# Cosine-similarity attention on one core: another order of the instructions, another polynomial for one chunk, other places for the root steps

## The chip, the cores and the metric

The kernel runs on one core of a Trainium2 chip. The core has five engines that run their own streams of instructions in order and wait for each other through semaphores: TensorE (PE, matrix products), VectorE (DVE), ScalarE (ACT, exponentials), GpSimd (POOL) and SyncE (SP, which here issues the DMA transfers). Data come from HBM to the on-chip SBUF by DMA; PE writes its products to PSUM. The metric is the device time of one execution in microseconds (us); the lower the better.

## The reference

Q, K and V are 8 batches × 12 heads × 512 rows × 64 columns, in 32-bit floating point; tau is 0.1.

```python
Q_norm = Q / (np.linalg.norm(Q, axis=-1, keepdims=True) + 1e-10)
K_norm = K / (np.linalg.norm(K, axis=-1, keepdims=True) + 1e-10)
scores = np.einsum('bhqd,bhkd->bhqk', Q_norm, K_norm) / tau
weights = np.exp(scores - np.max(scores, axis=-1, keepdims=True))
weights = weights / (np.sum(weights, axis=-1, keepdims=True) + 1e-10)
return np.einsum('bhqk,bhkd->bhqd', weights, V).astype(np.float32)
```

As the rows are normalised, a score is at most 10, and the kernel takes the exponential without subtracting the maximum.

## The kernel before

The 96 heads are taken in 48 pairs, numbered s = 0 to 47. The first and the last pair have special code. For each pair in between the steps are these; the short names are those of the program, and the lines those of the profile.

- SP loads Q and K of the pair (LD, L315) into one of 17 buffers `qk`, and V (LV, L318) into one of 9 buffers `vf`; much later it stores the result (ST, L582) from one of 8 buffers `ob`.
- POOL squares Q and K (SQ, L341), writes V as bf16 with a column of ones beside it (VC, L553), and scales most K by their roots (SCL with w = 1, L427).
- PE adds up squares in pairs of columns (SSQ, L358), and DVE reduces them to sums per row (RED, L365 and L369).
- DVE makes the reciprocal roots by Newton's method (NEW, L394 to L403): a first value from the bits of the sum, then multiplications. These steps are made for a group of pairs at once: groups of one, then two, then four pairs. The sums x and the intermediate t lie in PSUM (`nps`), the root y in SBUF (`ys`). DVE scales Q (SCL with w = 0, L427).
- PE transposes Q and K (TR, L433), and DVE copies them to SBUF (EVA, L441, `qt`).
- PE makes the scores in four chunks c of 128 keys (SCO, L532: two matmuls, one for each head, into one of two score buffers in PSUM). ACT takes the exponential of a chunk, 128 × 1024 values (EXP, L548, `et`).
- PE multiplies the weights with V (PV, L565: for each head four pieces of four matmuls each; the column of ones gives the sum of the weights). DVE takes the reciprocal (RCP, L576) and multiplies (NRM, L578) into `ob`.

One chunk, (43,3), isn't made by ACT: DVE and POOL compute its exponential as a polynomial in six steps (Y, L488 to L490), and its pair's Q is scaled by one more step on DVE (UNIT, L418) so that the polynomial works on a suitable unit.

In the head, before the first data have come, PE runs eight dummy matmuls (L191) on the eye matrix `ident` and on a zeroed operand `warm_in`, which DVE sets to zero (L195).

No loop sets the order in which an engine takes these steps. Each step is entered once in a list, with what it needs; `ORDER` then holds for each engine a sequence of numbers of that list, and the engine runs them in this sequence. So SP also holds back whatever stands behind a transfer whose buffer is not free yet. The numbers of buffers stand in `RINGS`.

Of the kernel before, what the change touches and what calls it, by code (L numbers as in the profile page):

```python
# [108 lines left out]
def bass_cosine_similarity_attention_kernel(  # L109
# [14 lines left out]

    R_QK, R_V, R_SQ, R_QN, R_QT, R_ET, R_O, R_X = RINGS
# [13 lines left out]
    ys = [sb(f"ys{i}", [128, 64], f32) for i in range(R_X)]  # L139
    xs = {g: sb(f"xs{g}", [128, 64], f32) for g in NORM_ON_ACT}  # L140
    rk = [sb(f"rk{i}", [128, 32], f32) for i in range(R_X)]
# [3 lines left out]
    warm_in = sb("warm_in", [128, SEQ], bf16)  # L145
# [5 lines left out]
    o_ps = [nc.alloc_psum_tensor(f"ops{b}", [128, 512], f32) for b in range(2)]  # L151
    t_ps = nc.alloc_psum_tensor("tps", [128, 2, NT, 128], bf16)
    x_ps = t_ps[:, :, :, :].rearrange("p w t x -> p (w t x)").bitcast(f32)
    t_k0 = o_ps[0][:, :].bitcast(bf16)[:, 0:SEQ].rearrange("p (t x) -> p t x", t=NT)
    n_ps = nc.alloc_psum_tensor("nps", [128, R_X, 160], f32)
# [16 lines left out]

    def src(x, s):
        b, h = divmod(2 * s, NHEAD)
        return x[b, h : h + 2].rearrange("h (p t) d -> p h (t d)", t=NT)

    def key(name, s, *rest):
# [9 lines left out]
        vb[:, :, :, :, DIM : DIM + 1].rearrange("p r c h o -> p (r c h o)"), 1.0))  # L187

    def warm(e):
        for k in range(WARM):  # L190
            last = e.matmul(out=o_ps[1][:, :], lhsT=ident[:, :], rhs=warm_in[:, :], start=True, stop=True)  # L191
        return last

    P.fill = lambda e, n: e.matmul(out=o_ps[1][:, 0:n], lhsT=ident[:, :], rhs=warm_in[:, 0:n], start=True, stop=True)
    P.add("wz", "dve", "sm_dve", -100, [], lambda e: e.memset(warm_in[:, :], 0.0))  # L195
    P.add("warm", "pe", "warm", -100, ["eye", "wz"], warm)
# [5 lines left out]
    def due_red(s):  # L202
        return due_sq(s) + 2.0
# [3 lines left out]
    off_of = {s: c for s, c in OFF}  # L207
    turn_user = {}
    for (s, c), (turns, _) in OFF.items():
        for h in range(2):  # L210
            turn_user.setdefault(turns[h], []).append((s, h))
# [10 lines left out]
    for s, w in sorted(early):  # L222
        session[s, w] = (w, due_red(s), before[w])
        before[w] = [("RED", s, w)]
# [6 lines left out]
    def head0(TF):  # L231
        for h in range(2):
            at = -100 + h
            x4 = [xs[0][:, 8 * w + 4 * h : 8 * w + 4 * h + 4] for w in range(2)]
            y4 = [ys[0][:, 8 * w + 4 * h : 8 * w + 4 * h + 4] for w in range(2)]
# [7 lines left out]
            r_ps = sc_ps[:, 1, 0:4] if h == 0 else n_ps[:, 0, 128:132]  # L243
# [42 lines left out]
    def new(g):  # L286
        if g <= 0:
            return []
        return [("NEW", g, 7)] if direct_r(g) else [("NEW", g, 6), ("NEW", g, 7)]
# [7 lines left out]
    def last_direct(s):  # L297
        d = [g for g in NORM_ON_ACT if g > 0]
        return [("NEW", max(d), 7 if direct_r(max(d)) else 6)] if d and group[s] not in NORM_ON_ACT and s < 12 else []

    def pair(s):
# [6 lines left out]
        for w, x in ((0, Q), (1, K)):  # L308
            if s == 0:
# [7 lines left out]
        P.add(("LV", s), "sp", "ld", s + VLAG, [key("VC", s - R_V)],  # L317
              lambda e: e.dma_start(out=vf[iv][:, :, :], in_=src(V, s)), slot=f"v{iv}")  # L318
# [30 lines left out]
        x2 = (xs[g][:, 0 : 2 * m] if acts else n_ps[:, g % R_X, 0 : 2 * m]).rearrange("p (w x) -> p w x", w=2)  # L349
        for w in range(2):  # L350
# [16 lines left out]
            else:  # L367
# [6 lines left out]
        rq_g, rk_g = n_ps[:, g % R_X, 128 : 128 + m], xs[g][:, m : 2 * m] if acts else rk[g % R_X][:, 0:m]  # L374
        rkd = n_ps[:, g % R_X, 128 + m : 128 + 2 * m] if acts else tg[:, m : 2 * m]
        on_dve = [i for i in range(first[g], first[g] + sizes[g]) if i in K_ON_DVE]
        free = [[("SCL", i, k) for i in range(first[g - R_X], first[g - R_X] + sizes[g - R_X])] if g > R_X else []
                for k in range(2)]
        reds = [("RED", i, w) for i in range(first[g], first[g] + sizes[g]) for w in range(2)]
        if s == first[g] and g in NORM_ON_ACT:  # L380
            at = NORM_ON_ACT[g]
            P.add(("LOG", g), "act", "ln", at, reds + ["eps"],
                  lambda e: e.activation(out=ys[g % R_X][:, 0 : 2 * m], in_=xs[g][:, 0 : 2 * m], func=ACT.Ln, bias=eps[:, :]))
            direct = direct_r(g)
            P.add(("NEW", g, 7), "act", "sm_act", at + 0.01, [("LOG", g)] + ([("SCL", first[g] - 1, w) for w in range(2)] if direct and g > 1 else [("NRMS", 0, 0, 1), ("SCL", 0, 0, 1)]),
                  lambda e: e.activation(  # L386
                      out=n_ps[:, g % R_X, 128 : 128 + 2 * m] if direct else xs[g][:, m : 2 * m],
                      in_=ys[g % R_X][:, 0 : 2 * m] if direct else ys[g % R_X][:, m : 2 * m], func=ACT.Exp, scale=-0.5)).own = True
            if not direct:
                P.add(("NEW", g, 6), "act", "sm_act", at + 0.005, [("LOG", g), ("SCL", 0, 0, 1)],  # L390
                      lambda e: e.activation(
                          out=n_ps[:, g % R_X, 128 : 128 + m], in_=ys[g % R_X][:, 0:m], func=ACT.Exp, scale=-0.5)).own = True
        elif s == first[g]:
            yx = lambda e: e.tensor_tensor(out=tg, in0=xg, in1=yg, op=ALU.mult)  # L394
            yyx = lambda e: e.scalar_tensor_tensor(  # L395
                out=tg, in0=tg, scalar=-0.5, in1=yg, op0=ALU.mult, op1=ALU.mult)

            def up(dst, lo, hi):
                return lambda e: e.scalar_tensor_tensor(
                    out=dst, in0=tg[:, lo:hi], scalar=1.5, in1=yg[:, lo:hi], op0=ALU.add, op1=ALU.mult)  # L400

            steps = [
                lambda e: e.tensor_scalar(  # L403
                    out=yg.bitcast(i32), in0=xg.bitcast(i32), scalar1=-0.5, scalar2=MAGIC,
                    op0=ALU.mult, op1=ALU.add),
                yx, yyx, up(yg, 0, 2 * m), yx, yyx, up(rq_g, 0, m), up(rk_g, m, 2 * m)]
            if on_dve:
                steps.append(up(tg[:, m : 2 * m], m, 2 * m))
            for k, step in enumerate(steps):
                needs = [("NEW", g, min(k, 6) - 1 if k < 8 else 7)] if k else reds + (free[1] if K_ON_DVE else [])  # L410
                if k == 0 and g == R_X:
                    needs += [("NRMS", 0, w, h) for w in range(2) for h in range(2)]
                if 6 <= k < 8:
                    needs += free[k - 6]
                P.add(("NEW", g, k), "dve", "new", TF - 4.9 - slack(s, M_NEW) + (M_STEP * (k - 7) if s > 8 else 0.23 * k), needs, step)

        if s in off_of:
            P.add(("UNIT", s), "dve", "new", TF - 3.0, [("NEW", g, 6)], lambda e: e.tensor_scalar(  # L418
                out=rq_g[:, c8 : c8 + 8], in0=rq_g[:, c8 : c8 + 8], scalar1=UNIT * inv_tau / math.log(2.0), scalar2=1.0,
                op0=ALU.mult, op1=ALU.mult))  # L420
        for w in range(2):
# [4 lines left out]
                  [("NEW", g, (7 if direct_r(g) else 6) if acts and dve else 6 + w + (dve and w))] + ([("UNIT", s)] if s in off_of and w == 0 else []) + ([("TR", 0, w, 0), ("TR", 0, w, 1)] if s == R_QN else [key("TR", s - R_QN, w)]),  # L426
# [26 lines left out]
    def last_step(s, c):  # L453
        return {"A": 5, "B": 4, "C": 5, "P": 6}[OFF[s, c][1]]

# [9 lines left out]
    def poly(s, c, at):  # L465

        turns, form = OFF[s, c]
# [20 lines left out]
        add = lambda o, x, v: lambda e: e.tensor_scalar(out=o, in0=x, scalar1=v, scalar2=1.0, op0=ALU.add, op1=ALU.mult)  # L488
        mul = lambda o, x, y: lambda e: e.tensor_tensor(out=o, in0=x, in1=y, op=ALU.mult)
        fused = lambda o, x, v, y: lambda e: e.scalar_tensor_tensor(out=o, in0=x, scalar=v, in1=y, op0=ALU.add, op1=ALU.mult)  # L490
        steps = [("pool", "yt", mul(z, z, z)), ("pool", "ys", add(w, z, a1)), ("pool", "yt", mul(w, w, w))]
        if form == "A":
            steps += [("pool", "ys", add(w, w, a2)), ("dve", "yd", fused(e_, z, a3, w)), ("dve", "ym", mul(e_, e_, p2))]
        elif form == "B":
            steps += [("dve", "yd", fused(z, z, a3, p2)), ("dve", "yd", fused(e_, w, a2, z))]
        elif form == "C":
            steps += [("pool", "ys", add(z, z, a3)), ("pool", "yt", mul(z, z, p2)), ("dve", "yd", fused(e_, w, a2, z))]
        else:
            steps += [("pool", "ys", add(z, z, a3)), ("pool", "yt", mul(z, z, p2)), ("pool", "ys", add(w, w, a2)), ("pool", "yt", mul(e_, w, z))]
        for j, (eng, kind, step) in enumerate(steps):  # L500
# [3 lines left out]
            if j == (4 if form == "A" else last_step(s, c)):  # L504
                needs += [key("PV", s - R_ET, h, NT - 1) for h in range(2)]
            P.add(("Y", s, j), eng, kind, at + 2 + 1.9 * j, needs, step)

    def rest(s):
        iq, iv, iqt, iet, io = (s % r for r in (R_QK, R_V, R_QT, R_ET, R_O))
        T0 = START + PERIOD * s  # L510
        last_pair = s == NP - 1
        for c in range(NT):
# [3 lines left out]
            if s == 0:  # L516
                for h in range(2):
# [7 lines left out]
                              out=et[iet][:, c, h, :], in_=sc_ps[:, c, :], func=ACT.Exp, scale=xs[0][:, 8 + 4 * h + c : 9 + 4 * h + c])).own = True  # L525
# [267 lines left out]
```

## Time and profile before

| | us |
|---|---|
| three runs | 190.22, 189.85, 191.28 |
| their median | 190.22 |
| the profiled execution (its span) | 190.9 |
| busy: PE, DVE, ACT, POOL | 175.9, 170.2, 182.7, 161.8 |

The profile is of one execution. "Busy" is the time in which an engine had an instruction running. A row of a timeline gives start, duration, engine, line, operation, what it writes and reads, and how many such instructions it joins; a bracket at its end is the time in which the engine stood idle ahead of it and what ended that. A row of a table of lines gives the busy time, the mean of one in nanoseconds, and the idle time ahead. A row of a table of windows gives the busy time of each engine in that stretch, and at its end the clock that PE was granted (1.00 is full speed), the share of the DMA engines that was busy, and the bytes per second. Matmul durations overlap, so the time that PE needs for one is best read from the starts of two neighbouring rows.

### The profile page before, as it was taken

Reading aid. Unit: us, or ns where it says so; the run is one execution under the profiler, and the core shown is the slowest. Engines: PE = TensorE matmul, PEld = TensorE weight load, DVE = VectorE, ACT = ScalarE, POOL = GpSimd, SP = SyncE. Lnnn points to the kernel's source line nnn. Section 1 sums busy time; section 2 is a strip of 40 time slices with the busy share of each in tenths; the row PEclk is TensorE's granted clock in tenths of the full one; section 3 lists DMA queues with packets and bytes.
Section 4 is the critical chain, followed back from the end, with each engine's and each line's share of the span. In section 5 each row is a group of like instructions: output and inputs, shape, how many; then the busy total and the mean of one; then the engine's idle time right before and its main releaser. Section 6 shows DMA issues by size and latency. Waiting matters only on the chain.

```text
span 190.9 us, 6650 instructions
## 1 busy us (share of the span) xinstructions
PE 175.9 (92%) x2705; PEld 109.4 (57%) x2705; DVE 170.2 (89%) x552; ACT 182.7 (96%) x215; POOL 161.8 (85%) x150
## 2 busy tenths in 40 slices
PE   7699699999999999999999999999999899897973
PEld 2355266666656666666566666556656565464642
DVE  2668999999999999999997998999999999988642
ACT  5678999999999999999999999999999999999994
POOL 5397898999999999999999999999999994793000
PEclk9958999999999999999999999999999999999998
DMA  5999999997999599999979999999950414000565
GB/s 162 344 348 349 350 348 372 365 297 250 268 351 337 169 260 320 357 366 369 380 277 272 351 377 364 354 379 384 365 194 5 165 58 165 3 0 3 193 197 165
DMA packets 52446, 50.76 MB, mean 266 GB/s; under 512 B 3136, under 2 KB 52416, under 8 KB 52416
## 3 DMA queue, kind: packets, MB, share of 16 engines
q1 hardware_dynamic: 51984, 50.02, 79.7%
q8 instruction: 21, 0.34, 0.8%
q10 hardware_dynamic: 432, 0.33, 0.5%
q14 instruction: 9, 0.07, 0.1%
HBM read 37.75 MB, written 12.58 MB: 264 GB/s over the span
## 4 chain that ended last, share of the span: by engine, by line
ACT 89%; PE 4%; DMA 3%; DVE 1%; issue 0%; SPq 0%
ACT et L548 88%; DMA qk<-in_Q_dram 3%; PE ops L358 2%; PE scps L521 1%; PE tps L433 1%; DVE qn L427 1%; PE scps L532 0%; SPq L312 0%; ACT et L543 0%; ACT sq L333 0%; ACT ob L608 0%; PE tps L270 0%; DVE qn L261 0%; DVE ob L612 0%; PE ops L593 0%
## 5 line engine op out<-in xcount | busy, mean ns | idle before, releaser
L548 ACT ACTIVATE et<-scps 128x1024 bf16<-128x1024 f32 x186 | 171.3, 1113 | 0.6 <-PE scps L532 0.4
L341 POOL TENSOR_TENSOR sq<-qk 128x1024 bf16<-128x1024 f32 x44 | 83.1, 1896 | 0.1
L532 PE MATMUL scps<-qt 64*128 64x512 bf16 x374 | 73.3, 387 | 6.3 <-ACT et L548 3.3
L565 PE MATMUL ops<-vb,et 128*128 128x65 bf16 x1504 | 72.8, 195 | 1.7 <-DVE ob L578 1.0
L565 PEld LDWEIGHTS ops<-vb,et 128*128 128x128 bf16 x1504 | 55.3, 98 | 30.9 <-issue 18.3
L427 POOL TENSOR_TENSOR qn<-qk,rk 128x512 bf16<-128x512 f32 x38 | 39.5, 1045 | 5.9 <-PE scps L532 3.7
L578 DVE TENSOR_TENSOR ob<-ops,rd 128x256 f32<-128x256 f32 x94 | 38.8, 418 | 0.7
L427 DVE TENSOR_TENSOR qn<-qk,nps 128x512 bf16<-128x512 f32 x56 | 37.2, 677 | 0.7 <-ACT nps L386 0.6
L433 PE MATMUL tps<-ident,qn 128*128 128x128 bf16 x376 | 34.3, 222 | 0.9 <-POOL qn L427 0.3
L441 DVE COPY qt<-tps 128x1024 bf16<-128x1024 bf16 x47 | 32.1, 682 | 0.4 <-PE tps L433 0.4
L532 PEld LDWEIGHTS scps<-qt 64*128 64x128 bf16 x374 | 18.2, 92 | 23.5 <-ACT et L548 9.6
L369 DVE TENSOR_REDUCE nps<-sq 128x8 f32<-128x512 bf16 x46 | 30.8, 682 | 0.8 <-POOL sq L341 0.7
L553 POOL TENSOR_SCALAR vb<-vf 128x512 bf16<-128x512 f32 x48 | 29.7, 630 | 0.1
L433 PEld LDWEIGHTS tps<-ident,qn 128*128 128x128 bf16 x376 | 21.9, 99 | 12.0 <-issue 5.4
L576 DVE RECIPROCAL rd<-ops 128x4 f32<-128x4 f32 x94 | 16.1, 174 | 6.6 <-PE ops L565 5.9
L358 PE MATMUL ops<-sq,ident 128*128 128x64 bf16 x384 | 20.0, 199 | 0.1
L358 PEld LDWEIGHTS ops<-sq,ident 128*128 128x128 bf16 x384 | 15.2, 101 | 4.3 <-issue 2.5
L365 DVE TENSOR_REDUCE nps<-ops 128x8 f32<-128x64 f32 x46 | 10.0, 218 | 0.9 <-PE ops L358 0.7
L394 DVE TENSOR_TENSOR nps<-nps,ys 128x32 f32<-128x32 f32 (+2 forms) x34 | 7.0, 207 | 0.4
L395 DVE SCALAR_TENSOR_TENSOR nps<-nps,ys 128x32 f32<-128x32 f32 (+2 forms) x34 | 7.0, 206 | 0.4
L335 POOL TENSOR_TENSOR sq<-qk 128x512 bf16<-128x512 f32 (+1 forms) x5 | 4.7, 956 | 3.2 <-DMA qk<-in_K_dram 2.8
L524 ACT ACTIVATE et<-scps,xs 128x512 bf16<-128x512 f32 x8 | 4.9, 682 | 0.3 <-PE scps L521 0.3
(66 smaller groups left out, 57.8 us busy)
## 6 DMA issues: line engine op xcount, KB each, us to landing
vf<-in_V_dram SPq DMA_DIRECT2D x48, 256.0 KB, 6.6
qk<-in_Q_dram SPq DMA_DIRECT2D x47, 256.0 KB, 5.5
qk<-in_K_dram SPq DMA_DIRECT2D x47, 256.0 KB, 6.3
out_dram<-ob SPq DMA_DIRECT2D x47, 256.0 KB, 5.7
qk<-in_Q_dram SPq DMA_DIRECT2D x2, 128.0 KB, 2.7
qk<-in_K_dram ACTq DMA_DIRECT2D x2, 128.0 KB, 2.8
out_dram<-ob SPq DMA_DIRECT2D x1, 128.0 KB, 1.7
out_dram<-ob SPq DMA_DIRECT2D x1, 64.0 KB, 1.6
```

Of the source, the lines that this page charges most:

```text
L341: lambda e: e.tensor_tensor(out=sqf, in0=data, in1=data, op=ALU.mult))
L358: last = e.matmul(out=o_ps[bank][:, 320:384], lhsT=ident[:, :], rhs=sq[iqs][:, 8 * w : 8 * w + 8, 8 * k : 8 * k + 8], start=(k == 0), stop ...
L369: lambda e, w=w, dst=dst: e.tensor_reduce(out=dst, in_=sq[iqs][:, 8 * w : 8 * w + 8, :], axis=AX.X, op=ALU.add))
L427: lambda e, w=w, r=r: e.tensor_tensor(out=qn[iqn][:, w].rearrange("p t h d -> p h t d"), in0=qk[iq][:, w].rearrange("p h (t d) -> p h t d" ...
L433: last = e.transpose(t_ps[:, w, t, :], qn[iqn][:, w, t].rearrange("p h d -> p (h d)"), ident[:, :])
L441: lambda e: e.tensor_copy(out=qt[iqt][:, :, :, :].rearrange("p w t x -> p (w t x)"), in_=t_ps[:, :, :, :].rearrange("p w t x -> p (w t x)")))
L532: last = e.matmul(out=sc_ps[:, 2 * b + h, :], lhsT=qt[iqt][64 * h : 64 * h + 64, 1, c, :], rhs=qt[iqt][64 * h : 64 * h + 64, 0, :, :], sta ...
L548: lambda e, c=c, b=b: e.activation(out=et[iet][:, c, :, :], in_=sc_ps[:, 2 * b : 2 * b + 2, :], func=ACT.Exp, scale=math.log(2.0) / UNIT i ...
L553: lambda e: e.tensor_scalar(out=vb[:, iq, :, :, 0:DIM].rearrange("p c h d -> p h c d"), in0=vf[iv][:, :, :].rearrange("p h (c d) -> p h c ...
L565: last = e.matmul(out=o_ps[h][:, 65 * t : 65 * t + 65], lhsT=et[iet][:, c, h, 128 * t : 128 * t + 128], rhs=vb[:, iq, c, h, :], start=(c = ...
L576: lambda e, h=h, grid=grid: e.reciprocal(out=rd[io][:, h, :], in_=grid[:, :, DIM]))
L578: lambda e, h=h, grid=grid: e.tensor_tensor(out=ob[io][:, h], in0=grid[:, :, 0:DIM], in1=rd[io][:, h, :].unsqueeze(2).to_broadcast([128, N ...
```

## The change

It has five parts.

1. *Warm-up.* Nine dummy matmuls in place of eight. Both operands are the constant of ones that the preamble sets up, so they wait neither for the eye matrix nor for a zeroed operand; the operand and its memset are gone. One later dummy of 256 columns is gone too.
2. *Newton's method.* The sums x and the intermediate t lie in SBUF (`xs`, `ts`), the root y in PSUM (`nps`). The step that made a second copy of K's root for DVE (step 8) is gone, and so is step 6 of a group whose K is scaled by DVE alone; in all there are nine steps fewer.
3. *The chunk off ScalarE.* The polynomial is another one, with five steps (three on POOL, two on DVE) in place of six (four on POOL). Its unit is put into the constants of the last Newton steps (`c_g`), for Q and K of the whole group of pair 43, and the exponentials of this group have the inverse factor as their scale; UNIT is gone.
4. *Buffers.* V's raw buffers are 8 in place of 9, in one tensor; V's bf16 buffers are 16 and have a ring of their own (before they were numbered as `qk`, 17), with the head ahead of the chunk in their layout. Each V is still cast alone. The two PSUM banks for PV are one tensor with two halves.
5. *Order.* SP, POOL, DVE and PE have other sequences in `ORDER`: in the head nearly the same, behind it new throughout. ACT's differs in its last steps only.

The diff, cut to its core:

```diff
-    vf = [sb(f"vf{i}", [128, 2, NT * DIM], f32) for i in range(R_V)]
-    vb = sb("vb", [128, R_QK, NT, 2, DIM + 1], bf16)
+    vf = sb("vf", [128, R_V, 2, NT * DIM], f32)
+    vb = sb("vb", [128, R_VB, 2, NT, DIM + 1], bf16)
...
-            last = e.matmul(out=o_ps[1][:, :], lhsT=ident[:, :], rhs=warm_in[:, :], start=True, stop=True)
+            last = e.matmul(out=o_ps[1], lhsT=one(128), rhs=one(SEQ), start=True, stop=True)
...
-    P.add("wz", "dve", "sm_dve", -100, [], lambda e: e.memset(warm_in[:, :], 0.0))
-    P.add("warm", "pe", "warm", -100, ["eye", "wz"], warm)
+    P.add("warm", "pe", f"warm{WARM}", -100, [], warm)
...
-        xg = n_ps[:, g % R_X, 0 : 2 * m]
-        tg = n_ps[:, g % R_X, 64 : 64 + 2 * m]
-        yg = ys[g % R_X][:, 0 : 2 * m]
+        xg, tg, yg = xs[g % R_X][:, 0 : 2 * m], ts[g % R_X][:, 0 : 2 * m], n_ps[:, g % R_X, 0 : 2 * m]
...
+        c_g = math.sqrt(UNIT * inv_tau / math.log(2.0)) if g in poly_groups else 1.0
...
+                1: yx, 2: yyx(1.0), 3: up(yg, 0, 2 * m, 1.0), 4: yx, 5: yyx(c_g), 6: up(rk_g, m, 2 * m, c_g),
+                7: up(yg, 0, 2 * m, c_g) if on_dve else up(rq_g, 0, m, c_g)}
...
-            P.add(("UNIT", s), "dve", "new", TF - 3.0, [("NEW", g, 6)], lambda e: e.tensor_scalar(
-                out=rq_g[:, c8 : c8 + 8], in0=rq_g[:, c8 : c8 + 8], scalar1=UNIT * inv_tau / math.log(2.0), scalar2=1.0,
-                op0=ALU.mult, op1=ALU.mult))
...
-        steps = [("pool", "yt", mul(z, z, z)), ("pool", "ys", add(w, z, a1)), ("pool", "yt", mul(w, w, w))]
-            steps += [("pool", "ys", add(w, w, a2)), ("dve", "yd", fused(e_, z, a3, w)), ("dve", "ym", mul(e_, e_, p2))]
+            ("pool", "yt", mul(z, z, z)),
+            ("pool", "ys", lambda e: e.tensor_scalar(out=w, in0=z, scalar1=a1, scalar2=a2, op0=ALU.add, op1=ALU.mult)),
+            ("pool", "yt", mul(w, w, z)),
+            ("dve", "yd", lambda e: e.scalar_tensor_tensor(out=e_, in0=w, scalar=a3, in1=z, op0=ALU.add, op1=ALU.mult)),
+            ("dve", "ym", mul(e_, e_, p2))]
...
-                      func=ACT.Exp, scale=math.log(2.0) / UNIT if s in off_of else inv_tau))
+                      func=ACT.Exp, scale=math.log(2.0) / UNIT if group[s] in poly_groups else inv_tau))
...
-RINGS = (17, 9, 6, 4, 4, 5, 8, 3)
+RINGS = (17, 8, 16, 6, 4, 4, 5, 8, 3)
...
-WARM = 8
+WARM = 9
...
-        "7 8 70 71 109 110 11 154 155 72 198 199 111 241 242 156 275 276 200 317 318 243 351 352 277 394 395 319 "
+        "6 7 69 70 108 109 10 151 152 71 195 196 110 423 237 238 153 465 197 314 271 272 348 313 347 541 239 424 "
```

The new order at the places of which the prediction speaks. First SP, before, from its 35th row on: the load of V into buffer `vf2`, the store of pair 0, and the loads of pairs 12, 13 and 14.

```order
L318 DMA vf2<-in_V_dram 128x2x256
L582 DMA out_0_dram<-ob0 128x2x256
L315 DMA qk12<-in_Q_dram 128x2x256
L315 DMA qk12<-in_K_dram 128x2x256
L315 DMA qk13<-in_Q_dram 128x2x256
L315 DMA qk13<-in_K_dram 128x2x256
L315 DMA qk14<-in_Q_dram 128x2x256
```

SP after, the rows that hold the same loads of pair 12 (`qk12`). The first row is pair 24's Q, which goes into buffer `qk7`, the buffer of pair 7; `ob1` is the store of pair 1.

```order
L342 DMA qk7<-in_Q_dram 128x2x256
L342 DMA qk15<-in_Q_dram 128x2x256
L342 DMA qk14<-in_Q_dram 128x2x256
L608 DMA out_0_dram<-ob1 128x2x256
L342 DMA qk14<-in_K_dram 128x2x256
L345 DMA vf<-in_V_dram 128x2x256
L342 DMA qk12<-in_K_dram 128x2x256
L342 DMA qk12<-in_Q_dram 128x2x256
```

Pair 12's Q was SP's 37th DMA row and is now its 45th; ahead of it stands a load for pair 24, which waits until pair 7's Q has been scaled.

SP after, further on: the store of pair 10 (`ob2`), K of pair 27 (`qk10`), K of pair 21 (`qk4`), two V, and Q of pair 21.

```order
L608 DMA out_0_dram<-ob2 128x2x256
L342 DMA qk10<-in_K_dram 128x2x256
L342 DMA qk4<-in_K_dram 128x2x256
L345 DMA vf<-in_V_dram 128x2x256 x2
L342 DMA qk4<-in_Q_dram 128x2x256
```

Before, pair 21's Q stood eight rows ahead of the store of pair 10; now it stands five behind it.

PE before, around the score of chunk (17,0), the fourth row from the end: `sq4` are the squares of pair 22, `sq3` those of pair 21, `et4` and `et0` the weights of pairs 14 and 15, `qt0` and `qt1` the Q and K of pairs 16 and 17.

```order
L532 MATMUL scps<-qt0 128x512 x2
L565 MATMUL ops1<-vb,et4 128x65 x16
L565 MATMUL ops0<-vb,et0 128x65 x4
L532 MATMUL scps<-qt1 128x512 x2
L358 MATMUL ops0<-sq4,ident 128x64 x8
L358 MATMUL ops1<-sq3,ident 128x64 x8
L532 MATMUL scps<-qt1 128x512 x2
```

PE after, the same place; the score of chunk (17,0) is the fourth row.

```order
L551 MATMUL scps<-qt0 128x512 x2
L385 MATMUL ops<-sq4,ident 128x64 x8
L587 MATMUL ops<-vb,et4 128x65 x8
L551 MATMUL scps<-qt1 128x512 x2
L587 MATMUL ops<-vb,et4 128x65 x8
L385 MATMUL ops<-sq3,ident 128x64 x8
L551 MATMUL scps<-qt1 128x512 x2
```

The sum of squares of pair 22 has moved from behind the score to ahead of it, and 8 of the 20 PV matmuls that stood ahead of the score remain there.

More of the change, by code (lines that the diff above doesn't have):

```diff
@@ L382, in pair @@
+        if s == first[g] and acts:
+            at, lo = NORM_ON_ACT[g], ya[g][:, 0 : 2 * m]
             P.add(("LOG", g), "act", "ln", at, reds + ["eps"],
[L383 to L388, printed above, removed]
@@ L407, in pair @@
[L407 to L410, printed above, removed]
-                if k == 0 and g == R_X:
[L412 to L415, printed above, removed]
@@ new lines, in pair @@
+            for k in news(g):
+                needs = [done] if k else reds + [("SCL", i, w) for i in past for w in range(2) if w == 0 or i in K_ON_DVE]
+                if k == 0 and g == R_X:
+                    needs += [("NRMS", 0, w, h) for w in range(2) for h in range(2)] + [("SCL", 0, 0, h) for h in range(2)]
+                if k == 6:
+                    needs += [("SCL", i, 1) for i in past if i not in K_ON_DVE]
+                done = ("NEW", g, k)
+                P.add(done, "dve", "new7" if k == 7 and on_dve else "new", TF - 4.9 - slack(s, M_NEW) + (M_STEP * (k - 7) if s > 8 else 0.23 * k), needs, steps[k])
```

178 lines of the change are left out of this document (104 added, 74 removed), and 160 rows, old and new, of the table ORDER.

## The prediction

> **What bounds the kernel now.** I read the page's busy shares and its chain of work first, then ScalarE's (ACT's) timeline for gaps, then the windows of the DMA queue, and last the rows around the places where the order changes.
>
> ```profile
> PE 175.9 (92%) x2705; PEld 109.4 (57%) x2705; DVE 170.2 (89%) x552; ACT 182.7 (96%) x215; POOL 161.8 (85%) x150
> ACT 89%; PE 4%; DMA 3%; DVE 1%; issue 0%; SPq 0%
> L548 ACT ACTIVATE et<-scps 128x1024 bf16<-128x1024 f32 x186 | 171.3, 1113 | 0.6 <-PE scps L532 0.4
> 40.16 5.64 ACT L548 ACTIVATE et<-scps 128x1024 bf16<-128x1024 f32 x6
> ```
>
> ACT is the bound: 182.7 of 190.9 us, 89% of the chain, nearly all of it the 186 large exponentials of L548. Undisturbed, six of them take 5.64 us; with 1.113 for the last that is (5.64 − 1.113)/5 = 0.905 us from one to the next. Over the whole stream it is (171.3 − 1.1)/185 = 0.920. So the stream holds 185 × 0.0145 = 2.7 us of small waits that the profile does not show as idle: scores that arrive a little late. That is all an order of instructions can win in the stream. What ACT loses outside it is in the head:
>
> ```profile
> 7.28 0.63 ACT L333 ACTIVATE sq<-qk 128x512 bf16<-128x512 f32 x1 [1.90 <-DMA qk<-in_Q_dram]
> 10.34 0.31 ACT L383 ACTIVATE ys<-xs,eps 128x16 f32<-128x16 f32 x1 [0.69 <-DVE xs L365]
> 14.09 0.69 ACT L524 ACTIVATE et<-scps,xs 128x512 bf16<-128x512 f32 x1 [0.31 <-PE scps L521]
> 15.18 5.83 ACT L548 ACTIVATE et<-scps 128x1024 bf16<-128x1024 f32 x6 [0.40 <-PE scps L532]
> ```
>
> 1.90 us wait on the loads of pair 1; 0.69 + 0.31 + 0.40 = 1.40 us come where the first two rows below show TensorE (PE) at a granted clock of 0.50.
>
> ```profile
> core 0: us, PE busy (x) PEld busy (x) DVE busy (x) ACT busy (x) POOL busy (x), PEclk, DMA share, GB/s
> 9.00:12.00 3.00, 2.97 (x29) 1.56 (x29) 1.96 (x5) 2.31 (x8) 2.79 (x3) 0.50 1.10 352
> 12.00:15.00 3.00, 3.00 (x28) 1.85 (x27) 2.20 (x11) 2.47 (x5) 2.92 (x5) 0.50 1.10 348
> 76.00:96.00 20.00, 19.47 (x320) 12.39 (x317) 19.54 (x66) 20.00 (x24) 20.00 (x20) 1.00 1.09 368
> 63.27:71.00 7.73, 7.73 (x133) 5.07 (x133) 7.70 (x30) 7.73 (x9) 7.73 (x7) 1.00 0.86 244
> SPq L582 <- DVE ob L578: 31.6, 8, 15.8
> 63.27 0.37 SPq L582 DMA_DIRECT2D out_dram<-ob  x1
> out_dram<-ob SPq DMA_DIRECT2D x1, 256.0 KB, 2.1
> ```
>
> The other rows are the DMA side: two windows, SP's waits, an issue on SP and what became of it (issue to landing, last column). A full queue moves 368 GB/s: one transfer of 262,144 bytes each 0.71 us. SP waits for stores' results (31.6 us in all); after one such stretch the store at 63.27 meets an empty queue and lands 2.1 us later, and in the 7.73 us from there the queue moves only 244 GB/s: 1.07 us a transfer. In this kernel such a stretch costs nothing, because what is loaded there is needed much later.
>
> **The change, part by part.**
>
> *PE's order.* One stretch shows what is to be had:
>
> ```profile
> 132.32 0.39 PE L532 MATMUL scps<-qt 64*128 64x512 bf16 x2
> 132.65 0.55 PE L565 MATMUL ops<-vb,et 128*128 128x65 bf16 x12
> 133.12 0.39 PE L532 MATMUL scps<-qt 64*128 64x512 bf16 x2
> 133.48 0.66 PE L565 MATMUL ops<-vb,et 128*128 128x65 bf16 x16
> 133.97 0.40 PE L358 MATMUL ops<-sq,ident 128*128 128x64 bf16 x8
> 134.30 0.39 PE L532 MATMUL scps<-qt 64*128 64x512 bf16 x2
> ```
>
> A pair of scores takes 0.33 us (132.32 to 132.65), 16 PV matmuls 0.49 (so 0.122 for four), eight sums of squares 0.33. Between two scores there is room for 0.905 − 0.33, about 0.58 us. Here 16 PV and eight sums stand between: 0.82 us, and the score comes 1.18 us after the last. Adding up the pieces over both whole orders by these prices, 44 gaps between scores of before are over 0.58, by 5.5 us together, and 14 of the new order, by 2.0. The trace shows 2.7 of the 5.5 as waits (the two score buffers absorb the rest), a share of 0.49; by the same share the new order keeps 1.0. Gain: 1.7 us; bounds 0 and 2.7.
>
> *The Newton steps, the folded scale and the sextic.*
>
> ```profile
> L394 DVE TENSOR_TENSOR nps<-nps,ys 128x32 f32<-128x32 f32 (+2 forms) x34 | 7.0, 207 | 0.4
> L399 DVE SCALAR_TENSOR_TENSOR nps<-nps,ys 128x16 f32<-128x16 f32 (+2 forms) x25 | 4.3, 181 | 0.1
> L399 DVE SCALAR_TENSOR_TENSOR rk<-nps,ys 128x16 f32<-128x16 f32 (+2 forms) x17 | 2.9, 172 | 0.1
> L418 DVE TENSOR_SCALAR nps<-nps 128x8 f32<-128x8 f32 x1 | 0.2, 164 | 0.0
> L488 POOL TENSOR_SCALAR xw<-xw 128x1024 f32<-128x1024 f32 x1 | 1.1, 1051 | 0.1
> ```
>
> DVE loses nine small root steps and the scale of one pair (L418), 9 × 0.18 + 0.16 = 1.8 us in 170, and the memset of the old warm-up operand. Where the operands lie (x and t in SBUF, y in PSUM, the reverse of before) moves a step by little: the same step into SBUF and into PSUM is 172 and 181 ns here, so for some 125 steps the bound is ±1.1 us of DVE. POOL loses one step of 1.05. None of it is on the chain (DVE 1%, POOL not in it); the cover is the ACT stream, gapless after 15.2. I take 0; bounds −0.5 (DVE is 89% busy) and +0.2.
>
> *The warm-up.*
>
> ```profile
> 1.41 3.59 PE L191 MATMUL ops<-warm_in,ident 128*128 128x512 bf16 x8 [1.41 <-POOL eps L184]
> 0.36 0.10 POOL L775 MEMSET const-bfloat16-1.0<- 128x1 bf16 x1
> 4.93 0.55 PE L272 MATMUL ops<-ident,qn 128*64 128x128 bf16 x4
> ```
>
> The constant is there at 0.46 instead of the eye at 1.35, so the nine dummies start up to 0.9 us earlier; at 3.59/8 = 0.45 each they take 4.04 and end between 4.5 and 5.4, where the first real work stood at 4.93. The head waits for the loads until 7.28 whatever PE does, so I take 0. Bounds by the half-clock stretch: −1.4 if full clock now covers the gaps at 10.34, 14.09 and 15.18, and +1.4, as much again, if the half clock comes earlier and takes in the head's transposes from 4.93 on (an estimate by symmetry, as no row shows it).
>
> *SP's order and the rings.* From its 13th DMA on, SP issues far-ahead loads and stores first, each with its late wait, and near ones behind. One that waits stops all behind it, and the queue runs dry. V's ring goes from 9 to 8 and V's casts are shuffled as well. I price the two clearest places and one longer one, with the trace's own times for the waits.
>
> ```profile
> 33.06 0.68 DVE L427 TENSOR_TENSOR qn<-qk,nps 128x512 bf16<-128x512 f32 x1
> 41.75 3.75 POOL L341 TENSOR_TENSOR sq<-qk 128x1024 bf16<-128x1024 f32 x2
> 45.46 1.04 POOL L427 TENSOR_TENSOR qn<-qk,rk 128x512 bf16<-128x512 f32 x1
> 46.30 0.66 PE L433 MATMUL tps<-ident,qn 128*128 128x128 bf16 x8
> 62.83 0.41 DVE L578 TENSOR_TENSOR ob<-ops,rd 128x256 f32<-128x256 f32 x1
> 71.45 1.89 POOL L341 TENSOR_TENSOR sq<-qk 128x1024 bf16<-128x1024 f32 x1
> 73.48 0.39 PE L532 MATMUL scps<-qt 64*128 64x512 bf16 x2
> ```
>
> Place A: the load of pair 24's Q waits for pair 7's scaling (ends 33.74), and pair 12's Q is the eighth from there: 33.74 + 2.1 + 7 × 1.07 = 43.3, against 41.75, when POOL began its squares (row of two, pairs 12 and 13). Behind them POOL scales pair 10's K, and PE's transposes of pair 10 stand just ahead of the score of chunk (9,3). All shift by 1.6, of which 0.1 is slack (the scaling ended 46.50): +1.5.
>
> Place B: the store of pair 10 waits for its result (63.24); the sixth transfer, counting this store, is pair 21's Q: 63.24 + 2.1 + 5 × 1.07 = 70.7. POOL then squares pairs 21 and 22, until 70.7 + 2 × 1.89 = 74.5. The new PE order puts pair 22's sum of squares ahead of score (17,0), which stood at 73.48 and before had it behind. With 0.33 for the sum and 0.24 for eight PV it must begin by 72.9: +1.6.
>
> Place C:
>
> ```profile
> 121.94 0.64 POOL L553 TENSOR_SCALAR vb<-vf 128x512 bf16<-128x512 f32 x1
> 133.00 0.42 DVE L578 TENSOR_TENSOR ob<-ops,rd 128x256 f32<-128x256 f32 x1
> ```
>
> The load of pair 38's V waits for pair 30's cast, which the new POOL order puts behind as much work as stood ahead of the cast that ended at 122.6. The store of pair 23 is twelfth behind it: 122.6 + 2.1 + 7 × 1.07 + 4 × 0.71 = 135.0. Pair 31's result, at 133.00, needs that buffer, and PV of pair 32, ahead of score (33,2), needs that result: +2.0, with 0.2 of slack +1.8.
>
> Three more places of this kind (stores of pairs 9 and 20, the load of pair 37's K) I put at an estimated 0.6 each, between 0 and place B's 1.6: +1.8. Together 1.5 + 1.6 + 1.8 + 1.8 = 6.7; bounds 0 (all land in time) and 9.7.
>
> A page's rule would deny this term. In the Trainium skill, "DMA: Bandwidth & Descriptors", section "Anatomy of one DMA", a DMA costs a fixed part of about 2 us plus its bytes at 436 GB/s, and the same page puts HBM at about 358 GB/s per core; neither makes transfers slow after a dry stretch, and by it this term would be 0 and the time 188.5. The 2.1 us for the lone store agrees with it roughly, the 244 GB/s do not.
>
> **Sum.** 190.9 − 1.7 + 0 + 0 + 6.7 = 195.9 against the profiled execution. The median of the three runs (190.22) is 0.7 under it: 195.2.
>
> **Rivals.**
>
> *Transfers land in time (other side: faster or the same).* If a queue that fills again runs at 0.71 at once, place A is 33.74 + 2.1 + 4.97 = 40.8, before 41.75; B is 63.24 + 2.1 + 3.55 + 3.78 = 72.7, before 72.9; C is 122.6 + 2.1 + 7.8 = 132.5, before 133.0. All hidden, and only PE's 1.7 is left: 188.5. It decides at (41.75 − 33.74 − 2.1)/7 = 0.84 us a transfer for A and at (72.9 − 3.78 − 65.34)/5 = 0.76 for B. For it: 368 GB/s in the full window. Against: the 244 after 63.27, 1.07.
>
> *The change doesn't do what it says.* The two score buffers already absorb the crowded gaps, so PE's order wins nothing, and the loads are hidden: 190.2. For it: only 0.6 us of idle time is shown ahead of L548. Against: 0.920 beside 0.905.
>
> *The clock in the head.* −1.4 or +1.5 by the bounds above, on top of PE's gain: 187.1 or 189.9 with hidden loads. For it: the clock is granted at 0.50 in the two head windows although the warm-up came just before. Against: nothing in those windows is changed by the edit itself. In the Trainium skill, "TensorE: Matmul & The Clock Gate", Part 1, the gate looks at free-running windows of 3.4 us, one of them idle taking full clock back; by that an earlier warm-up may fall on either side of a window's end, with the one bound or the other, and no row here tells which.
>
> **How the numbers follow.** Late loads 0.57, centred on 195.2, its own range 192 to 199; loads in time with PE's gain 0.23 (188.5); no effect 0.13 (190.2); the clock deciding 0.07. The predicted time is the likeliest, 195.2. The range takes in the two other cases below and the larger bound above: 188.0 to 199.0. About 1% (1.9 us) is what a measurement can tell from no change. Faster than 188.3: somewhat under half of the second case, and most of the fourth, 0.15. Slower than 192.1: nearly all of the first and a little of the fourth, 0.57. The rest, 0.28.
>
> **What would show it.** PE's step: the mean distance of the L548 stream in gapless stretches falls from 0.920 towards 0.911. SP's step: ACT idle of 1 to 2 us near 47, 74 and 135 us, on scores whose chain goes through POOL's squares to a qk load; SP waits before it and GB/s below 260 after it. If ACT is gapless there, the DMA term is wrong and the time is near 188.5. The head: PEclk in 9 to 15 us, and whether the gaps at 10.34, 14.09 and 15.18 remain. DVE's busy time should fall by about 2 us, POOL's by 1, with no trace in the span. A DVE or POOL that releases ACT elsewhere would make the prediction wrong in a way that I have not priced.

## The result and the profile after

The changed kernel takes 204.67 us (median of 4 runs, 202.39 to 206.44) against 190.64 us of the kernel before (4 runs, 189.85 to 191.28): the ratio is 1.065, with an interval of 1.057 to 1.072. The profiled execution has a span of 203.9 us, 13.0 more than the 190.9 of before. Some executions of these kernels run a stretch at half clock and take longer (of the 33 timed runs of before beside the experiments, the 24 with a mean clock above 0.99 have a median of 190.2 us, the 9 others 191.9), so the ratios compare the faster executions alone and are not quotients of the medians.

The page of the changed kernel: the busy shares, the bytes per second in 40 slices of the span, the chain by engine, and the row of the large exponentials (now L567).

```profile
PE 179.1 (88%) x2705; PEld 112.0 (55%) x2705; DVE 170.2 (83%) x541; ACT 184.1 (90%) x215; POOL 161.2 (79%) x149
GB/s 180 334 350 351 351 351 150 253 350 363 305 334 334 290 366 377 295 143 351 353 373 25 263 237 342 311 253 349 363 50 267 5 102 281 86 0 3 103 126 239
POOL 32%; ACT 20%; DMA 16%; SPq 9%; PE 9%; DVE 8%; issue 4%; POOLq 0%; DVEq 0%
L567 ACT ACTIVATE et<-scps 128x1024 bf16<-128x1024 f32 x186 | 173.0, 1106 | 12.6 <-PE scps L551 12.2
```

ACT does the same work as before, but it now stands idle for 12.6 us ahead of the exponentials, where it was 0.6. The chain, which was ACT for 89%, is now 32% POOL, 20% ACT, 16% DMA and 9% SP, so a good part of it runs through transfers and through POOL's work on what they bring. The GB/s have holes (150, 143, 25, 50) where SP held back. DVE's busy time has not fallen at all and POOL's by 0.6, where the prediction said 2 and 1.

ACT's timeline shows where the idle time is (start, duration, number of exponentials; in brackets the idle time ahead and its releaser). The first row is the whole stream of before, the others are the stream after:

```profile
15.18 171.46 ACT L548 ACTIVATE et<-scps 128x1024 bf16<-128x1024 f32 x186 [0.40 <-PE scps L532]
12.62 5.78 ACT L567 ACTIVATE et<-scps 128x1024 bf16<-128x1024 f32 x6
18.95 5.68 ACT L567 ACTIVATE et<-scps 128x1024 bf16<-128x1024 f32 x6 [0.55 <-PE scps L551]
25.01 4.92 ACT L567 ACTIVATE et<-scps 128x1024 bf16<-128x1024 f32 x5 [0.38 <-PE scps L551]
30.79 14.87 ACT L567 ACTIVATE et<-scps 128x1024 bf16<-128x1024 f32 x16 [0.86 <-PE scps L551]
46.60 1.96 ACT L567 ACTIVATE et<-scps 128x1024 bf16<-128x1024 f32 x2 [0.94 <-PE scps L551]
49.45 26.95 ACT L567 ACTIVATE et<-scps 128x1024 bf16<-128x1024 f32 x29 [0.88 <-PE scps L551]
78.67 29.66 ACT L567 ACTIVATE et<-scps 128x1024 bf16<-128x1024 f32 x32 [2.27 <-PE scps L551]
110.02 2.15 ACT L567 ACTIVATE et<-scps 128x1024 bf16<-128x1024 f32 x2 [1.69 <-PE scps L551]
112.67 1.02 ACT L567 ACTIVATE et<-scps 128x1024 bf16<-128x1024 f32 x1 [0.51 <-PE scps L551]
114.13 17.52 ACT L567 ACTIVATE et<-scps 128x1024 bf16<-128x1024 f32 x19 [0.44 <-PE scps L551]
132.44 11.14 ACT L567 ACTIVATE et<-scps 128x1024 bf16<-128x1024 f32 x12 [0.79 <-PE scps L551]
145.99 1.02 ACT L567 ACTIVATE et<-scps 128x1024 bf16<-128x1024 f32 x1 [2.41 <-PE scps L551]
147.52 50.73 ACT L567 ACTIVATE et<-scps 128x1024 bf16<-128x1024 f32 x55 [0.51 <-PE scps L551]
```

The stream begins at 12.62 (before: 15.18, 2.6 later) and ends at 147.52 + 50.73 = 198.25, so it lasts 185.6 us; what follows lasts 5.7. Before, its last row ended at 186.65, so it lasted 171.5, with 4.3 behind it. The sum: −2.6 in the head, +14.2 in the stream, +1.4 at the end, 13.0 together.

Each wait followed back from the score to what came last (the "stall" is the distance of two starts less 0.905 us, a little more than the idle time in the bracket):

| score | stall, us | what it waited for in the end | predicted |
|---|---|---|---|
| (2,2), (4,0) | 0.67, 0.53 | K of pairs 5 and 6, behind Q of pairs 10 and 11 | none |
| (5,1) | 0.97 | DVE's result for pair 1, behind work on pair 7, whose squares POOL made after it had waited for K of pair 6 | none |
| (9,1), (9,3) | 1.09, 1.00 | Q of pair 12 (place A) | 1.5 |
| (17,0) | 2.63 | Q of pair 21 (place B) | 1.6 |
| (25,0); (25,2), (25,3) | 1.80; 0.62, 0.55 | V of pair 35, 16 transfers behind K of pair 37 (place D); then a lowered clock | 0.6 |
| (30,2) | 1.05 | store of pair 20, behind K of pair 46 (place E) | 0.6 |
| (33,2); (33,3) | 2.55; 0.63 | store of pair 23, behind V of pair 38 (place C); then a lowered clock | 1.8 |
| two more | 0.68 | V of pair 24, and PE's own order | none |

So the mechanism stands where it was forecast. At place B it can be read in single rows: the store of pair 10, POOL's wait for pair 21's Q, PE's wait for the squares, and the score.

```profile
64.91 0.38 SPq L608 DMA_DIRECT2D out_dram<-ob  x1
73.84 3.74 POOL L368 TENSOR_TENSOR sq<-qk 128x1024 bf16<-128x1024 f32 x2 [2.68 <-DMA qk<-in_Q_dram]
77.64 0.41 PE L385 MATMUL ops<-sq,ident 128*128 128x64 bf16 x8 [2.56 <-POOL sq L368]
78.24 0.39 PE L551 MATMUL scps<-qt 64*128 64x512 bf16 x2
```

From the store's issue to the landing that freed POOL (73.77) pass 8.9 us, where the forecast had 2.1 + 5 × 1.07 = 7.5.

Place D in the same way: the issue of pair 37's K, POOL's wait for V of pair 35 (it landed at 104.53), the squares behind that cast, PE's wait for them, the score of (25,0), and that of (25,2).

```profile
87.35 0.37 SPq L342 DMA_DIRECT2D qk<-in_K_dram  x1
104.61 0.62 POOL L575 TENSOR_SCALAR vb<-vf 128x512 bf16<-128x512 f32 x1 [1.73 <-DMA vf<-in_V_dram]
105.19 3.74 POOL L368 TENSOR_TENSOR sq<-qk 128x1024 bf16<-128x1024 f32 x2
108.99 0.41 PE L385 MATMUL ops<-sq,ident 128*128 128x64 bf16 x8 [1.83 <-POOL sq L368]
109.59 0.39 PE L551 MATMUL scps<-qt 64*128 64x512 bf16 x2
110.49 0.61 PE L551 MATMUL scps<-qt 64*128 64x512 bf16 x2
```

The two profiles differ in the head's clock (0.50 from 8.7 to 15.5 us before, full clock after), so the 2.6 us that the head is shorter can't be put down to the change from this pair alone; the experiments below take that up.

### The profile page after: what moved, and what is told of

Its sections match the earlier page's. It is cut to its first block, busy times and chain, and to the rows that moved or that the text cites. A ratio compares the mean times of both kernels' runs of the same rounds, so it can differ in the third digit from the quotient of the medians.

```text
span 203.9 us, 6659 instructions
## 1 busy us (share of the span) xinstructions
PE 179.1 (88%) x2705; PEld 112.0 (55%) x2705; DVE 170.2 (83%) x541; ACT 184.1 (90%) x215; POOL 161.2 (79%) x149
## 4 chain that ended last, share of the span: by engine, by line
POOL 32%; ACT 20%; DMA 16%; SPq 9%; PE 9%; DVE 8%; issue 4%; POOLq 0%; DVEq 0%
ACT et L567 20%; POOL sq L368 20%; DMA vf<-in_V_dram 11%; POOL qn L451 7%; DMA out_dram<-ob 5%; SPq L342 5%; POOL vb L575 5%; PE ops L587 4%; SPq L345 3%; PE scps L551 3%; DVE ob L604 2%; DVE qt L465 1%; DVE qn L451 1%; SPq L608 1%; DVE xs L396 1%
## 5 line engine op out<-in xcount | busy, mean ns | idle before, releaser
L567 ACT ACTIVATE et<-scps 128x1024 bf16<-128x1024 f32 x186 | 173.0, 1106 | 12.6 <-PE scps L551 12.2
L587 PE MATMUL ops<-vb,et 128*128 128x65 bf16 x1504 | 77.8, 197 | 4.2 <-DVE ob L604 3.8
L587 PEld LDWEIGHTS ops<-vb,et 128*128 128x128 bf16 x1504 | 58.7, 99 | 35.2 <-issue 21.5
L457 PE MATMUL tps<-ident,qn 128*128 128x128 bf16 x376 | 33.1, 221 | 1.8 <-DVE qn L451 0.9
L396 DVE TENSOR_REDUCE xs<-sq 128x8 f32<-128x512 bf16 x46 | 30.7, 674 | 2.0 <-POOL sq L368 2.0
L392 DVE TENSOR_REDUCE xs<-ops 128x8 f32<-128x64 f32 x46 | 9.9, 216 | 8.0 <-PE ops L385 7.7
L426 DVE SCALAR_TENSOR_TENSOR nps<-ts,nps 128x32 f32<-128x32 f32 (+3 forms) x34 | 6.6, 195 | 0.3
L422 DVE SCALAR_TENSOR_TENSOR ts<-ts,nps 128x32 f32<-128x32 f32 (+2 forms) x34 | 6.6, 193 | 0.4
L419 DVE TENSOR_TENSOR ts<-xs,nps 128x32 f32<-128x32 f32 (+2 forms) x34 | 6.5, 191 | 0.3
```

The source lines that it names most:

```text
L396: lambda e, w=w, dst=dst: e.tensor_reduce(out=dst, in_=sq[iqs][:, 8 * w : 8 * w + 8, :], axis=AX.X, op=ALU.add))
L457: last = e.transpose(t_ps[:, w, t, :], qn[iqn][:, w, t].rearrange("p h d -> p (h d)"), ident[:, :])
L567: lambda e, c=c, b=b: e.activation(out=et[iet][:, c, :, :], in_=sc_ps[:, 2 * b : 2 * b + 2, :], func=ACT.Exp, scale=math.log(2.0) / UNIT i ...
L587: last = e.matmul(out=o_ps[h][:, 65 * t : 65 * t + 65], lhsT=et[iet][:, c, h, 128 * t : 128 * t + 128], rhs=vb[:, ivb, h, c, :], start=(c ...
```

## The experiments

All kernels ran beside the kernel before. Ratios are to it, with intervals.

**The orders of before in the changed kernel.** SP, POOL, DVE and PE get the sequences of the kernel before; the last two root steps of a group stand side by side.

```
-RINGS, warm-up, root steps, polynomial: new;  ORDER: new
+RINGS, warm-up, root steps, polynomial: new;  ORDER sp, pool, dve, pe: as before
```

> The changed kernel with the sequences of the kernel before on SP, POOL, DVE and PE; warm-up, Newton steps, sextic and rings stay new. Theory (SP's new order makes transfers late: the stalls of ACT above 0.25 us sum to 14.8 us in the profile after and 0.2 before; the head is 2.6 us shorter by the earlier warm-up): no stall at a transfer, the head's gain stays, so about 190.6 - 2.6 = 188.0 us. Rival 1 (the stalls come from Newton in PSUM, or from V's rings of 8 and 16): they stay, over 200. Rival 2 (the head's gain belongs to the new order): 190.6.

192.52 us, ratio 1.012 (1.006 to 1.018). The stalls are gone but for one of 0.56 us, at (27,3), behind the store of pair 17, and two of about 0.3. So most of the loss sits in the orders. The head's gain is not in the time, against the theory: its profile starts the stream at 12.25 us, but a kernel with the old warm-up starts it at 12.68 (e4 below). The 1.2% that are left are not placed with certainty: beside the profile of e3, which has the orders of before too, the stream is 1.8 us longer (173.0 for 171.2) and what follows it 0.8 (5.1 for 4.3). See e7.

**SP's order alone, sorted by need.** Everything of the changed kernel stays, and only the sequence of SP is new.

```
 sp, first 12 DMAs: as after
-sp, the rest: as after
+sp, the rest: by max(time when the buffer is free, first use - 10 us)
```

> The changed kernel with SP's sequence alone sorted anew: after the first 12, each transfer stands at the time when its buffer is free, or 10 us before its first use if that is later; POOL, DVE, PE and ACT keep the new sequences. Theory (SP's order alone makes the transfers late): the 13.5 us of stalls whose chain runs back to a transfer go, 204.7 - 13.5 = 191.2, and as the waits at 30.8 and 57.0 us (1.25 us) may go too and PE stays warm, 188 to 191. Rival (the new sequences of POOL, DVE and PE stall ACT by themselves and the transfers are only the last link): above 197.

191.33 us in 10 runs, ratio 1.002 (0.998 to 1.006), where 188 to 191 was expected. ACT's timeline of this kernel:

```profile
12.95 171.06 ACT L567 ACTIVATE et<-scps 128x1024 bf16<-128x1024 f32 x186
183.68 1.36 ACT L562 ACTIVATE et<-scps 128x512 bf16<-128x512 f32 x3
```

All 186 exponentials run without a gap. With POOL, DVE and PE in the new order this took nothing but another sequence of the same transfers: given these orders of the other engines, SP's order makes the whole loss. No run has SP's new order beside the old orders of the others, and at place B the new place of pair 22's sum on PE takes part, so what SP's order would cost there stays open. The run also measures the rest of the change: with SP mended, the kernel is as fast as before, and no faster. PE's new order brings little: the stream took 171.3 us of busy time before and 171.06 here.

**The new warm-up alone, in the kernel before.**

```diff
-            last = e.matmul(out=o_ps[1][:, :], lhsT=ident[:, :], rhs=warm_in[:, :], start=True, stop=True)
+            last = e.matmul(out=o_ps[1][:, :], lhsT=one(128), rhs=one(SEQ), start=True, stop=True)
-WARM = 8
+WARM = 9
```

> The kernel before with nothing but the new warm-up: nine dummy matmuls of the constant, without waits, and no memset of the old operand. Theory (the earlier warm-up leaves the clock at full speed from 9 to 15 us, which is worth the gaps of 1.4 us and some of the rest): 188.0 to 189.2, PEclk 1.00 from 9 to 15. Rival (the head's gain was that pair 1's first load landed at 5.49 in place of 7.25, which is chance of a run): 190.6 with PEclk 0.50 there.

190.36 us in 10 runs, ratio 1.000 (0.996 to 1.004): no gain, where 188.0 to 189.2 was expected. Its profile has the full clock in the head:

```profile
9.00:12.00 3.00, 2.40 (x38) 1.38 (x34) 2.34 (x8) 2.83 (x8) 2.81 (x3) 1.00 1.09 358
12.00:15.00 3.00, 2.67 (x47) 1.62 (x44) 2.86 (x15) 3.00 (x6) 2.92 (x4) 1.00 1.11 349
```

In it the stream starts at 13.05 us, 2.1 earlier than in the profile of before. But the profile of e4, with the old warm-up, starts it at 12.68 with full clock in the head. The profiles of e7 and e10, with the new warm-up, have half clock there (from 9.1 to 12.6 and from 7.6 to 11.0 us). So a head at full clock is 2 to 2.6 us shorter with either warm-up, and the new one doesn't make sure of it.

**The orders of after in the kernel before**, with V's raw ring of 8.

```
-RINGS = (17, 9, 6, 4, 4, 5, 8, 3);  ORDER: as before
+RINGS = (17, 8, 6, 4, 4, 5, 8, 3);  ORDER sp, pool, dve, pe: as after
```

> The kernel before with the changed kernel's sequences on SP, POOL, DVE and PE, and V's raw ring of 8 that they need; warm-up, Newton steps, polynomial stay old. Theory (the orders make the loss): 190.6 + 14 = 204.6, or up to 207 with the old head; stalls of ACT at the same scores (9,1), (9,3), (17,0), (25,0), (30,2), (33,2). Rival (the loss needs the new Newton steps or the new vb ring): under 196.

202.95 us (204.6 to 207 expected), ratio 1.065 (1.059 to 1.072): the whole loss, with no other part of the change than the orders and that ring. It stalls at the same scores ((9,1), (9,3), (17,0), (25,0), (30,2), (33,2)). And its profile, though it has the old warm-up, starts the stream at 12.68:

```profile
12.68 2.88 ACT L548 ACTIVATE et<-scps 128x1024 bf16<-128x1024 f32 x3
```

**Place by place.** Five kernels move one or more transfers in SP's sequence of the changed kernel, and nothing else.

```
e6: -store 10, K 27, K 21, V 20, V 19, Q 21
    +K 27, K 21, V 20, V 19, Q 21, store 10                     (B)
e5: e6, and
    -Q 24, Q 15, ..., K 12, Q 12        +K 12, Q 12, Q 24, Q 15, ...   (A)
    -V 38, V 39, ..., store 26, store 23   +store 23, V 38, V 39, ...  (C)
e8: e5, and
    -K 37, V 23, ..., V 35              +V 23, ..., V 35, K 37         (D)
    -K 46, ..., V 30, store 20          +store 20, K 46, ..., V 30     (E)
e9: D alone
e10: -Q 10, K and Q 5, ..., Q 11, ..., K 7, K and Q 6   +5, 6 first, then Q 10, Q 11, K 7
```

> The changed kernel with place B alone mended (the store of pair 10 behind pair 21's Q). Theory: 204.7 - 2.6 = 202.1 us, (17,0) without a stall, the others as before. Rival (SP is behind as a whole): 204 or more.

> The changed kernel with three places of SP's sequence mended and nothing else: pair 12's K and Q ahead of pair 24's Q (place A), the store of pair 10 behind pair 21's Q (place B), the store of pair 23 ahead of pair 38's V (place C). Theory (each place costs what ACT's stalls there show: A 1.09 + 1.00, B 2.63, C 2.55 + 0.63 us): 204.7 - 7.9 = 196.8 us, and no stall above 0.25 at the scores (9,1), (9,3), (17,0), (33,2). Rival (SP is behind as a whole, so that what is gained at one place is lost at the next): above 201, with new or longer stalls.

> As e5_repair_abc, with two more places mended: pair 37's K behind pair 35's V, and the store of pair 20 ahead of pair 46's K. Theory (these two cost 1.80 + 0.62 + 0.55 and 1.05 us): 196.8 - 4.0 = 192.8 us, 1.5 above the sequence sorted by need. Rival (SP is behind as a whole): above 199.

> The changed kernel with one place mended: pair 37's K behind pair 35's V (place D, which the prediction priced at 0.6 us among three others). Theory (the place costs what ACT's stalls at (25,0), (25,2), (25,3) show, 1.80 + 0.62 + 0.55, the last two at a lowered clock): 204.7 - 3.0 = 201.7 us and no stall above 0.5 at these scores. Rival (the mend only moves the wait, as in e8_repair_five): 204 or more, with a new stall within 20 us.

> The changed kernel with the first loads in the order of their pairs: Q of pairs 10 and 11 and K of pair 7 behind pair 6, where no transfer waits for anything. Theory (two full-speed loads ahead of their turn cost 0.67 + 0.53 us at (2,2) and (4,0), which the prediction left out): 204.7 - 1.2 = 203.5 us and no stall above 0.25 before (5,1). Rival (these stalls are in PE's order and not in the loads): they stay, 204.7.

| kernel | us | ratio (interval) | theory, us | gained (by the ratios), us | what follows |
|---|---|---|---|---|---|
| e6, B | 201.42 | 1.050 (1.043 to 1.056) | 202.1 | 2.9, expected 2.6 | holds: no stall at (17,0); 0.82 appears at (19,2), behind the store of pair 9, and the stalls at the other places change too |
| e5, A, B, C | 196.37 | 1.028 (1.021 to 1.034) | 196.8 | 7.1, expected 7.9 | holds; 0.33 is left at (9,3) |
| e8, A to E | 195.98 | 1.026 (1.019 to 1.034) | 192.8 | 0.2 more than e5, expected 4.0 | fails |
| e9, D alone | 203.14 | 1.063 (1.056 to 1.070) | 201.7 | 0.3, expected 3.0 | fails in the time, though no stall is left at (25,0) to (25,3) |
| e10, first loads | 204.02 | 1.071 (1.065 to 1.077) | 203.5 | −1.1, expected 1.2 | not decided by the time |

The gains are differences to the ratio of the changed kernel, 1.065, times 190.5 us; with these intervals such a difference is uncertain by about 2 us.

In e9 the stretch around place D is gapless as expected, and the next rows of ACT's timeline show what took its place:

```profile
99.66 24.13 ACT L567 ACTIVATE et<-scps 128x1024 bf16<-128x1024 f32 x26
124.74 3.77 ACT L567 ACTIVATE et<-scps 128x1024 bf16<-128x1024 f32 x4 [0.95 <-PE scps L551]
```

At 124.74 stands score (29,2), which had no stall in the changed kernel: it waits for a result that waits for the store of pair 19, which took 6.2 us from issue to landing here and 4.6 in the changed kernel. In e8 the same score stalls by 1.22 us. So A, B and C together gain about what their stalls show, while D and E bring nothing that can be measured, and a store that cost nothing before now holds ACT; why it lands later is not shown. For e8 there was less to win than the theory had: in the profile of e5, with D and E left as they were, their stalls are 0.78 and 1.00 us, not 4.0.

In e10 the stalls at (2,2) and (4,0) are gone, that at (5,1) falls from 0.97 to 0.32, and 0.90 us appears at (5,3), behind K of pair 10. That fits the first loads as the cause, but one profile does not prove it: the stalls at (2,2) and (4,0) are also missing in that of e5, where these loads stand as in the changed kernel.

**The orders and the rings of before**, to find the 1.2% of e1.

```diff
-RINGS = (17, 8, 16, 6, 4, 4, 5, 8, 3)
+RINGS = (17, 9, 17, 6, 4, 4, 5, 8, 3)
```

> As e1_old_orders, with the rings of the kernel before for V (9 raw buffers, 17 of bf16), so that only warm-up, Newton steps, polynomial and layout stay new. Theory (the 1.2% that e1 lost come from the smaller V ring, with which the old sequence of SP stands longer): 190.6 us, no stall behind the store of pair 17. Rival (they come from the new Newton steps or their places among the old order): 192.5 as e1.

194.12 us, ratio 1.011 (1.003 to 1.019), so about 1% is lost as in e1, against the theory. The stall at the store of pair 17 is gone, which fits the ring as its cause. Whether the 1% comes from the new root steps or from their places among the old orders stays open.

## Why the prediction went wrong, point by point

The side was right and the mechanism was the one named, but 204.67 lies above the range (188 to 199): the forecast put the change at 5.0 us over the median of before, and it was 14.0 by the medians, 12.3 by the ratio.

- *SP's order: +6.7, measured +14.2 in the stream and +1.4 in the tail (with SP sorted by need the tail is 4.4, against 4.3 before).* This is the step that failed, as a size; its upper bound, 9.7, was too low as well. The places that it lists cost 11.9 us by their stalls: place A 2.1 for 1.5, B 2.6 for 1.6, C 3.2 for 1.8, E 1.05 for 0.6, D 3.0 for 0.6; the store of pair 9 cost nothing that shows. The term called "three more places" failed most: 1.8 for all, and 3.0 at the load of pair 37's K (place D) alone. What stands behind that load was not counted: V of pair 35 is the 17th transfer from there, landing 17.2 us after the first issue, which is longer than place C (12 transfers, 13.0 us), and C was counted. Of D and C, 1.8 us are the lowered clock behind the wait, for which the sum has no term. Outside the list were the first loads (1.2), score (5,1) (0.97), and the tail (1.4).
- *The price of a transfer after a dry stretch, 1.07 us.* Nearly right: less 2.1 us for the first, the trace after gives 1.17 at A, 1.35 at B and 1.36 at E, and the longer rows C and D 0.99 and 0.94. The rival by which all would have landed in time is refuted: at the full queue's 0.71 us, place B's Q would have landed 2.1 + 5 × 0.71 = 5.7 us after the store's issue, and it took 8.9. The rule that the prediction set beside it, from "Anatomy of one DMA" in "DMA: Bandwidth & Descriptors" of the Trainium skill, is a fit per DMA for those that GpSimd issues. What failed here is its use for a row of transfers that SP issues, and not the fit, which no run here tests.
- *PE's order: −1.7.* Most of the gain is not there. The mean distance of the exponentials, which was to fall from 0.920 us towards 0.911, is 0.918 with SP mended (e2): 185 × 0.013 = 2.4 us of small waits are left, where the forecast kept 1.0. Counted from the starts in the trace, the whole stream lasts 171.5 us in the profile of before, 171.2 with the same orders in e3, and 171.1 in e2: a gain of 0.1 to 0.4 us. The step that carried the share of 0.49 over to the new order's gaps failed. The rival by which the score buffers take up nearly all of it was right on this term.
- *Newton, scale, sextic: 0.* Holds: e2 contains them all and equals the kernel before. The step in SBUF is a little faster (L422, 193 ns for 206), not slower. DVE's busy time did not fall, but with the new orders on both sides it is 172.0 us with the old steps (e4) and 170.2 with the new: the 1.8 forecast are there, and the new orders took them back.
- *Warm-up: 0.* Holds in the time (e3). The bound of −1.4 for the head was too small for a profile at full clock: the stream starts 2.6 earlier, and there pair 1's load landed at 5.49 instead of 7.25 as well. The +1.5 among the rivals is a slip for the +1.4 of the bounds.
- *The step from the profile to the median, −0.7.* It sets a time (190.22) against a span (190.9), and a time is about 2 us more than the span of the same execution (190.24 and 188.4 in e2). It cost the forecast nothing, since what is forecast is the median plus the terms.

## What to carry to other kernels

A queue that runs in order pays for every early wait with all that stands behind it: before moving a transfer ahead, write down the wait it brings and count the transfers up to the first one with a near use, for every such place and not for the clearest alone. Sorting the transfers by the later of "buffer free" and "first use less a lead" took the whole loss away and needed no cost model of the transfers. Mending the places one at a time gave less than the sum of their stalls: in e9 and e8 the next late store, which had cost nothing, held ACT in their place.

## What the runs showed of the hardware

*The clock goes by fixed windows, and half a window of waiting is enough.* In all 12 profiles the changes of the granted clock lie on a grid of 3.41 us. Six windows of the changed kernel on that grid (columns as before; the second number is PE's busy time, the last but two the granted clock):

```profile
72.92:76.34 3.42, 2.16 (x31) 1.25 (x30) 2.49 (x12) 3.42 (x4) 2.50 (x2) 1.00 1.08 368
76.34:79.75 3.41, 2.11 (x40) 1.50 (x40) 1.66 (x8) 1.14 (x3) 3.41 (x4) 1.00 1.09 375
107.06:110.47 3.41, 1.58 (x32) 1.12 (x30) 1.41 (x5) 1.72 (x3) 3.41 (x4) 1.00 0.11 37
110.47:113.88 3.41, 3.41 (x36) 2.10 (x34) 2.73 (x6) 2.62 (x3) 3.41 (x5) 0.50 0.45 116
141.19:144.60 3.41, 1.37 (x16) 0.72 (x14) 1.38 (x7) 2.39 (x3) 3.41 (x2) 1.00 1.09 379
144.60:148.02 3.42, 3.21 (x40) 2.19 (x40) 2.17 (x5) 1.52 (x2) 2.52 (x3) 0.50 0.97 338
```

PE's longest wait in these, 2.56 us at place B, falls on two windows, 1.26 and 1.31 idle, and the clock stays. The wait of 1.83 at place D lies in one window, and the next window runs at half clock; so does the one after 2.04 idle at C. There stand the further stalls at (25,2), (25,3) and (33,3), 1.8 us together; a pair of scores takes 0.61 us in the row of (25,2) and 0.39 in that of (25,0). Over all profiles every window with 1.6 us or more of idle PE was followed by half clock. Of the windows at full clock with less than 1.26 us none was, but for the one in which the stream of e7 ends (1.16), and those between went either way. In the head of before the half clock stayed for a second window, though PE was idle for 0.1 us of the first. In the Trainium skill, "TensorE: Matmul & The Clock Gate", Part 1, the windows are free-running and 3413 ns long, which agrees. By the same part the clock falls after an idle window, and by its section "Why this matters for your kernels" a gap of about 3 us does it; here less was enough.

*A lone transfer can take twice as long.* A store that meets an empty queue lands after 2.1 to 2.2 us in most places, but the one of pair 44 took 4.5 in the profiles before and after alike. After, nothing was on the way when it was issued; before, it stood behind three stores (issue to landing, last column; the second row is the queue that loads instructions, in the changed kernel from 196.5 to 197.6 us):

```profile
out_dram<-ob SPq DMA_DIRECT2D x1, 256.0 KB, 4.5
q8 instruction: 1, 0.02, 5.4%
```

In 11 of the 12 profiles it took 3.7 to 4.6 us, and a 16 KB load of instructions ended 1.0 to 1.5 us before it landed. In the twelfth, e8, it took 2.5, though such a load began 2.0 us after the issue there as it did in the changed kernel. The store of pair 22, which meets an empty queue too, is a second case: 2.1 us in the changed kernel, where no such load falls between issue and landing, and 3.5 to 4.4 in e4, e5, e6, e8 and e9, where one began 1.1 to 1.8 us after the issue. No run here moves the load of instructions, so that the one delays the other is likely by these cases and not shown.
